# Recording the attention of both layers and emitting it on five engines in a planned order

## The chip, the core and the metric

The kernel runs on one core of one Trainium2 chip. The metric is the device time of one execution in microseconds (us). Before the change three runs took 1944.56, 1949.97 and 1951.2 us; their median is 1949.97 us. A fourth execution, taken with the hardware profiler, took 1945.29 us, and all rows of the trace come from it. The engines are TensorE (PE; its weight loads are shown as PEld), VectorE (DVE), ScalarE (ACT), GpSimd (POOL) and SyncE (SP), which issues the DMAs here.

## The reference, cut to what matters

Two layers of a trunk over 512 latent tokens and a prefix of 256 context tokens, with 1024 channels. In each layer:

```python
h  = modulate(rms_norm(x, norm1[l]), sh1, sc1)
na_q, na_k, na_v, gq, gk, gv, ga, gb = split(h @ w_in[l])     # one projection, eight parts
ya = na_latent(...)      # 8 heads: 8x16 windows on the 64-wide grid + all context keys, bias, softmax
yb = gqa_latent(...)     # 8 query heads on 2 key heads: rotary, normalised q and k, softmax over all keys
x  = x + g1 * ((sigmoid(ga) * (ya @ w_pa) + sigmoid(gb) * (yb @ w_pb)) @ w_o)
x  = x + g2 * swiglu(modulate(rms_norm(x, norm2[l]), sh2, sc2))
```

In the first layer the context tokens go through the same steps, with attention of their own; in the second layer they give keys and values alone.

## The kernel before, in words

Each fp32 operand is split in a high and a low half (`wh`/`wl` for weights, `h`/`hl` for activations, `pth`/`ptl` for transposed softmax weights), and each product is three matmuls. A weight block is loaded by SP into a ring of four buffers (`wr`, line 355), cast to `wh` on ACT (line 369) and subtracted to `wl` on GpSimd (line 371).

The attention stage of a layer is `mixing` (line 1385). It has a main thread, `attend` (line 1213), and fillers. The main thread goes through items; an item is two blocks of 128 queries of a head. Its steps are: scores (PE into the PSUM tile `sc`, one buffer of three banks), a minimum over each row (DVE, `TENSOR_REDUCE` at line 1048, or the fused add and minimum at line 1178 for windows), the exponential (ACT, line 1056 or 1180), the reciprocal of the row sum and the scaling (`soften`, lines 1009 and 1010, DVE), transposition (PE into `tp`), the split of the transposed tile (`split_t`: `pth` on ACT at line 1016, `ptl` on DVE at line 1017), the product with the values (PE into `y`), and its `join` (ACT line 1024, DVE line 1027). `tp`, `y`, `st` and `rb` share a PSUM ring of three buffers; the projections `pj` and `pv` have a ring of two. The fillers are the projections that the items and the later gates need: `na_q`, `na_k`, `na_v`, `gqa_q`, gates. Each ends in an evacuation of its PSUM tile by ACT and DVE, such as `sq`/`kg` (lines 815 and 816) or `qh`/`ql` (lines 990 and 991).

PE's order comes from the class `Flow` (line 148). While the program is being built, it walks the main thread, adds up PE's time in a clock, and lets fillers run until the time at which the main thread's next step is expected to be ready. The expected time comes from `Flow.go` (line 168), which books durations of the table `RATE` (line 96) on three lines for ACT, DVE and GpSimd. The instructions are issued to the framework at once. The whole stage stands in `manual_schedule(engines={PE})` (line 1516): PE keeps the order of issue, and the framework's own scheduler orders DVE, ACT, GpSimd and SP, across the stage and its neighbours. Each engine carries out its own instructions in order.

After the stage come `merge` (the gates, the products `pp` with `w_pa` and `w_pb`; its first operands `yb` are read back through DRAM and halved at lines 396 and 397), `out_proj`, and the feed-forward part, whose steps are ordered by hand on PE, DVE and ACT. The same merge computes modulation vectors beside its products (line 452, on `crow`, which line 444 and 445 prepare).

## Time and profile before

| | us |
|---|---|
| runs | 1944.56, 1949.97, 1951.2 (median 1949.97) |
| the profiled execution | 1945.29 |
| its span, first to last instruction | 1943.5 |
| PE busy | 1912.1 |
| attention stage of layer 0, about | 70 to 430 of the span |
| attention stage of layer 1, about | 1122 to 1452 of the span |

In rows of the profile, a matmul's duration overlaps the next one's, so an engine that is fed all the time shows 100% busy; "idle before" is the time between the end of the engine's last instruction and the start of this one, put down to the instruction that released it. Names stand as out<-in; L1017 is line 1017 of the kernel before.

### The profile page before, as it was taken

To read this page: it belongs to the slowest core of one execution; us is meant where nothing else is said; L and a number is where in the kernel's file an instruction comes from. 1 tells how busy PE (TensorE), PEld (TensorE's weight loads), DVE (VectorE), ACT (ScalarE), POOL (GpSimd) and SP (SyncE) were. 2 spreads that over 40 slices of the span, in tenths; PEclk is the share of its full clock that TensorE was granted. 3 is DMA by queue.
4 is the path that set the end of the run, shared out by engine and by line. 5 is a ranking of instruction groups with operands and counts; after the bars stand their busy time and mean duration, and the time that the engine had idled before them with its cause. 6 is when DMAs were issued, how large, how long until landed. Compare 5 with 4: busy or idle time off the path is not lost.

```text
span 1943.5 us, 31493 instructions
## 1 busy us (share of the span) xinstructions
PE 1912.1 (98%) x12298; PEld 1775.8 (91%) x12298; DVE 1470.0 (76%) x2802; ACT 943.0 (49%) x1822; POOL 226.6 (12%) x131
## 2 busy tenths in 40 slices
PE   8999999999999999999999998999999999999998
PEld 8989999998899999999999888889988999999998
DVE  7468887769877888786868577888657687877785
ACT  5466666652336533342424346666553355544553
POOL 0332222213300000000000012322300000000000
PEclk9999999999999999999999999999999999999999
DMA  8121112235562233334344411112235532332332
GB/s 328 44 65 48 47 64 63 77 105 182 170 217 87 66 120 122 117 116 133 131 141 143 143 62 55 47 60 64 73 102 173 201 109 77 98 120 88 103 97 83
DMA packets 71669, 210.85 MB, mean 108 GB/s; under 512 B 8544, under 2 KB 10720, under 8 KB 71520
## 3 DMA queue, kind: packets, MB, share of 16 engines
q1 hardware_dynamic: 71520, 208.84, 33.5%
q8 instruction: 96, 1.57, 0.3%
q14 instruction: 53, 0.43, 0.1%
HBM read 196.75 MB, written 6.82 MB: 105 GB/s over the span
## 4 chain that ended last, share of the span: by engine, by line
PE 69%; DVE 4%; issue 1%; ACT 1%; POOL 0%; DMA 0%; DVEq 0%; POOLq 0%; ACTq 0%
PE po L384 21%; PE qu L1740 14%; PE pj L384 11%; PE qv L1740 7%; PE pp L384 4%; PE qc L1740 3%; PE pf L384 3%; PE pv L957 1%; PE sc L1040 1%; PE y L1076 1%; PE tp L1066 1%; PE y L1203 1%; PE sc L1167 1%; PE tp L1191 1%; DVE m L1048 0%
## 5 line engine op out<-in xcount | busy, mean ns | idle before, releaser
L1740 PE MATMUL qu<-r,w 128*128 128x384 f32 (+1 forms) x1872 | 295.9, 310 | 0.3
L1740 PEld LDWEIGHTS qu<-r,w 128*128 128x128 f32 x1872 | 281.0, 190 | 4.9 <-DVE tt L2219 3.7
L384 PE MATMUL pj<-h,wh 128*128 128x512 f32 (+1 forms) x704 | 257.4, 366 | 3.3 <-ACT kg L816 1.7
L384 PE MATMUL pj<-h,wl 128*128 128x512 f32 (+1 forms) x704 | 247.6, 352 | 1.2 <-POOL wl L371 1.2
L384 PE MATMUL pj<-hl,wh 128*128 128x512 f32 (+1 forms) x704 | 247.0, 351 | 0.0
L369 ACT ACTIVATE wh<-wr 128x1024 fp32r<-128x1024 f32 (+1 forms) x131 | 124.6, 954 | 168.9 <-issue 43.5
L1603 ACT ACTIVATE w<-wr 128x512 fp32r<-128x512 f32 x234 | 145.4, 625 | 107.6 <-DVE wr L2183 36.1
L384 PE MATMUL po<-ph,wh 128*128 128x512 f32 (+1 forms) x576 | 197.5, 343 | 0.0
L384 PE MATMUL po<-ph,wl 128*128 128x512 f32 (+1 forms) x576 | 196.9, 342 | 0.0
L384 PE MATMUL po<-pl,wh 128*128 128x512 f32 (+1 forms) x576 | 196.3, 341 | 0.0
L371 POOL TENSOR_TENSOR wl<-wr,wh 128x1024 fp32r<-128x1024 f32 (+1 forms) x67 | 151.0, 2258 | 370.8 <-ACT wh L369 364.7
L1595 DVE SCALAR_TENSOR_TENSOR x<-po,G,x 128x256 f32<-128x256 f32 (+3 forms) x168 | 99.2, 596 | 101.0 <-PE po L384 100.0
L1607 DVE TENSOR_TENSOR w<-wr,w 128x512 fp32r<-128x512 f32 x234 | 159.4, 686 | 11.9 <-ACT w L1603 11.0
L384 PEld LDWEIGHTS pj<-h,wl 128*128 128x128 f32 x704 | 133.3, 189 | 19.7 <-POOL wl L371 1.6
L1740 PE MATMUL qv<-r,w 128*128 128x384 f32 (+1 forms) x936 | 150.7, 310 | 0.3 <-ACT tt L1746 0.3
L384 PEld LDWEIGHTS pj<-h,wh 128*128 128x128 f32 x704 | 133.7, 190 | 17.4 <-ACT kg L816 1.9
L384 PEld LDWEIGHTS pj<-hl,wh 128*128 128x128 f32 x704 | 134.0, 190 | 13.5
L1740 PEld LDWEIGHTS qv<-r,w 128*128 128x128 f32 x936 | 141.2, 190 | 0.5 <-ACT tt L1746 0.5
L1016 ACT ACTIVATE pth<-tp 128x512 fp32r<-128x512 f32 x176 | 103.2, 595 | 65.1 <-PE tp L1066 36.8
L512 POOL TENSOR_TENSOR rs<-rs,expo 128x2 f32<-128x2 f32 (+2 forms) x8 | 6.2, 773 | 1100.4 <-DVE rs L511 1100.4
L1017 DVE TENSOR_TENSOR ptl<-tp,pth 128x512 fp32r<-128x512 f32 x176 | 119.4, 684 | 18.4 <-ACT pth L1016 17.0
L384 PEld LDWEIGHTS po<-ph,wl 128*128 128x128 f32 x576 | 108.3, 188 | 14.3 <-DVE wl L1911 0.4
(255 smaller groups left out, 4325.2 us busy)
## 6 DMA issues: line engine op xcount, KB each, us to landing
wr<-wfi SPq DMA_DIRECT2D x88, 512.0 KB, 3.3
wr<-wmodT SPq DMA_DIRECT2D x84, 512.0 KB, 3.4
wr<-win SPq DMA_DIRECT2D x68, 512.0 KB, 3.3
wr<-wfo SPq DMA_DIRECT2D x64, 256.0 KB, 2.7
wr<-wo SPq DMA_DIRECT2D x26, 512.0 KB, 3.9
wr<-wp SPq DMA_DIRECT2D x32, 256.0 KB, 3.0
x<-x SPq DMA_DIRECT2D x16, 384.0 KB, 6.7
wr<-wmod SPq DMA_DIRECT2D x12, 512.0 KB, 7.6
```

Source lines behind the costliest of these rows:

```text
L369: nc.scalar.activation(hi, raw, AF.Copy)
L371: (eng or nc.gpsimd).tensor_tensor(lo, raw, hi[:].bitcast(F32), op=ALU.subtract)
L384: nc.tensor.matmul(ps[:, : b - a], u[:, c], v[k][:, a:b], start=(k == 0 and i == 0), stop=(k == nk - 1 and i == 2),)
L957: nc.tensor.matmul(ps[:, t * 256 : t * 256 + 256], a[k][:, tok], b[:, c], start=(k == 0 and i == 0), stop=(k == KB - 1 and i == 2))
L1016: nc.scalar.activation(hi, tp, AF.Copy)
L1017: nc.vector.tensor_tensor(lo, tp, hi[:].bitcast(F32), op=ALU.subtract)
L1040: nc.tensor.matmul(s[:, lo:up], qt[:, b * P : (b + 1) * P], kk[k][:, lo:up], start=(k == 0 and (b % 2 == 0 or lo > 0)), stop=(k == 1), ski ...
L1066: nc.tensor.transpose(tp[:, (2 * j + b) * P : (2 * j + b + 1) * P], ps_[b][:, (k + j) * P : (k + j + 1) * P], self.ident)
L1595: self.nc.vector.scalar_tensor_tensor(x[j][:, f:u], ps[:, f - a : u - a], self.G[l][i][:, s, j : j + 1], x[j][:, f:u], op0=ALU.mult, op1=A ...
L1603: self.nc.scalar.activation(t[:, :n], src, AF.Copy)
L1607: self.nc.vector.tensor_tensor(t[:, n : 2 * n], src, t[:, :n].bitcast(F32), op=ALU.subtract)
L1740: nc.tensor.matmul(banks[bank], u[:, c], v, start=(first and k == 0 and i == 0), stop=(k == kn - 1 and i == 2), skip_group_check=True)
```

## The change: what it does

For both layers (`all=True` in the table `PLAN`) the stage is first recorded and then emitted. While it is recorded, each call to an engine goes to `Plan.add`, which notes the instruction, its tiles, a duration from `Plan.cost` and which earlier instructions it has to follow. `Flow.go` now answers from the recorded ends. A tile in SBUF is compared by region; a tile in PSUM counts as one region, and all accesses to it by different engines keep the recorded order. `Plan.emit` then walks all recorded instructions: PE and SP keep their recorded order, while for ACT, DVE and GpSimd it takes among the instructions that can start first the one that is due first, where the due time is worked back from the PE instruction that needs it. It issues all of them by planned start, with five engines in `manual_schedule`. A scaling, subtraction or copy on DVE between SBUF tiles is not begun in the plan while GpSimd runs, and a GpSimd instruction is put off where such a DVE instruction is due earlier. The engines' instructions are the same in number, kind and shape. All instructions of the two stages bear line 541 in the changed kernel, since they are issued there.

The core of the diff:

```diff
-         busy=12, ctx=0.0, vat=(1, 1), load=2, qt=2, rx=2, slow=(1.1, 1.2, 1), banks="gst", lead=(2, 1, 2), quiet=0.0, spared=0),
+         busy=12, ctx=0.0, vat=(1, 1), load=2, qt=2, rx=2, slow=(1.1, 1.2, 1), banks="gst", lead=(2, 1, 2), quiet=0.0, spared=0, all=True),
...
     def go(self, t, *ops):
+        if self.plan:
+            return self.plan.go(t, ops)
...
+    def passed(self, v):
+        self.clock = max(self.clock + v, self.plan.pe if self.plan else 0.0)
...
+class Plan:
+    HOPS = dict(p=0.055, v=0.035, a=0.035, g=0.078, s=0.1)
+    TAIL = dict(p=-0.16, v=0.085, a=0.105, g=0.07, s=-2.2)
...
+    def go(self, t, ops):
+        flow, seen = self.flow, set()
+        for e, n in ops:
+            fixed, each, on = RATE[e]
+            if on in self.recent:
+                t = max(t, self.recent.pop(on))
+                seen.add(on)
+            elif on not in seen:
+                t += 0.05 + fixed + 0.08 + n * each
+        return t + flow.hop - 0.05
...
+    def region(ap, psum):
...
+        return (0, P, 0, 3 * S) if psum else (p, p + ap.ap[0][1], f, g)
...
+    def cost(self, lane, op, aps, kw, psum):
...
+        if lane == "s":
+            return n * aps[0].ap[0][1] * 4 / 0.34e6
+        if lane == "g":
+            return 0.31 if op == "memset" else 0.5 + n * 0.142 if n <= 16 else 0.14 + n * 0.0022
+        if lane == "a":
+            return 0.16 + n * 0.00088 + 0.08 * scaled + 0.1 * ("accum_out" in kw)
...
+        return 0.15 + n * (0.0006 if one else 0.00105) + 0.06 * (op == "scalar_tensor_tensor" and not psum)
...
+    def emit(self):
...
+        for i in reversed(range(n)):
+            o = ops[i]
+            due[i] = o["at"] if o["lane"] == "p" else min(
+                [due[j] - o["cost"] - 0.05 for j in then[i] + frees[i]], default=o["at"] + 15.0)
...
+            return max(t, clock["g"] - 0.07) if ops[i]["shared"] else t
...
+        for i in sorted(range(n), key=lambda i: (start[i], i)):
+            ops[i]["run"](*ops[i]["args"], **ops[i]["kw"])
...
-            with tc.manual_schedule(engines={mybir.EngineType.PE}):
+            if PLAN[l]["all"]:
+                nc.plan = flow.plan = Plan(flow)
                 flow.run(self.attend(items))
+                nc.plan = None
+                every = ("PE", "DVE", "Activation", "Pool", "SP")
+                with tc.manual_schedule(engines={getattr(mybir.EngineType, e) for e in every}):
+                    flow.plan.emit()
```

What stands where is shown at three places. The first is DVE in layer 1, where an item of the second query heads meets the evacuation of a key projection (`k<-pj`). `m<-sc` is the row minimum of one of the item's two blocks, `ptl` the split of a transposed tile of the item before. Before:

```order
L1017 TENSOR_TENSOR ptl_13250<-tp_13244,pth_13249 128x512
L936 TENSOR_TENSOR k_13321<-pj_13168,k_13321 64x512
L1048 TENSOR_REDUCE m_13271<-sc_13262 128x1
L1048 TENSOR_REDUCE m_13273<-sc_13262 128x1
L936 TENSOR_TENSOR k_13324<-pj_13168,k_13324 64x512
L1054 TENSOR_TENSOR m_13271<-m_13271,hr_12267 128x1
L1017 TENSOR_TENSOR ptl_13293<-tp_13287,pth_13292 128x512
L1054 TENSOR_TENSOR m_13273<-m_13273,hr_12267 128x1
```

and in the changed kernel, at the same projection (`k<-pj`, 64x512) of that layer:

```order
L541 TENSOR_TENSOR k_12124<-pj_12105,k_12124 64x512
L541 TENSOR_TENSOR q_12101<-qg_11985,q_12101 64x512
L541 TENSOR_TENSOR k_12125<-pj_12105,k_12125 64x512
L541 TENSOR_REDUCE m_12128<-sc_12127 128x1
L541 TENSOR_TENSOR ptl_12136<-tp_12134,pth_12135 128x512
L541 TENSOR_REDUCE m_12129<-sc_12127 128x1
L541 TENSOR_TENSOR m_12128<-m_12128,hr_12067 128x1
L541 TENSOR_TENSOR m_12129<-m_12129,hr_12067 128x1
L541 TENSOR_TENSOR y_12089<-y_12137,ys_12138 64x256
L541 TENSOR_TENSOR ptl_12141<-tp_12139,pth_12140 128x512
```

A `ptl` now stands between the two minima of an item, and the key's second half ahead of them; before, both minima and the key's second half stood ahead of the next `ptl`.

The second place is ACT at the beginning of layer 1, where the key projection of the context, `pj` 128x256, is evacuated by `sq` and `kg`. `wh` is the cast of a weight block for a later projection. Before:

```order
L1352 ACTIVATE kk_11969<-kg_11714 64x512 x2
L1352 ACTIVATE kk_11975<-kg_11714 64x512 x2
L369 ACTIVATE wh_11998<-wr_11996 128x1024
L990 ACTIVATE qh_12027<-pj_12002 64x448
L369 ACTIVATE wh_12104<-wr_12102 128x1024
L815 ACTIVATE sq_11715<-pj_12039 128x256
L816 ACTIVATE kg_11714<-pj_12039,gain_sb 128x256
L990 ACTIVATE qh_12027<-pj_12002 64x64
L990 ACTIVATE qh_12033<-pj_12002 64x448
```

and after:

```order
L541 ACTIVATE kk_11848<-kg_11714 64x512 x2
L541 ACTIVATE v_11812<-tv_11828 128x4x64
L541 ACTIVATE q_11851<-qg_11818 64x512
L541 ACTIVATE qh_11842<-pj_11841 64x448
L541 ACTIVATE wh_11839<-wr_11838 128x1024
L541 ACTIVATE qh_11842<-pj_11841 64x64
L541 ACTIVATE q_11852<-qg_11818 64x512
L541 ACTIVATE qh_11844<-pj_11841 64x448
L541 ACTIVATE sq_11715<-pj_11850 128x256
L541 ACTIVATE qh_11844<-pj_11841 64x64
L541 ACTIVATE kg_11714<-pj_11850,gain_sb 128x256
L541 ACTIVATE wh_11854<-wr_11853 128x1024
```

The two casts `wh` that stood right around the query halves have moved: one stays ahead of `sq`, the other is behind `kg`, and parts of `qh` and `q` stand ahead of `sq` instead.

The third place is DVE at the end of layer 0's stage, where the framework's own order takes over again. `y<-y` is the last join of the attention, `lo<-yb` halves the first operands of the merge, `junk` and `crow` prepare the modulation vectors. Before:

```order
L1027 TENSOR_TENSOR y_4757<-y_4989,ys_4994 64x256
L397 TENSOR_TENSOR lo_5113<-yb_5104,hi_5112 128x768
L397 TENSOR_TENSOR lo_5117<-yb_5106,hi_5116 128x768
L397 TENSOR_TENSOR lo_5121<-yb_5108,hi_5120 128x768
L397 TENSOR_TENSOR lo_5125<-yb_5110,hi_5124 128x768
L444 SCALAR_TENSOR_TENSOR junk_5170<-junk_5170,crow_5169 128x1024
L445 TENSOR_SCALAR crow_5169<-junk_5170 128x1024
L444 SCALAR_TENSOR_TENSOR junk_5170<-junk_5170,crow_5169 128x1024
L445 TENSOR_SCALAR crow_5169<-junk_5170 128x1024
L1585 SCALAR_TENSOR_TENSOR mb_5134<-gt_1454,pp_5135 128x512
```

and after:

```order
L541 TENSOR_TENSOR y_1500<-y_1548,ys_1549 64x256
L716 SCALAR_TENSOR_TENSOR junk_5170<-junk_5170,crow_5169 128x1024
L717 TENSOR_SCALAR crow_5169<-junk_5170 128x1024
L716 SCALAR_TENSOR_TENSOR junk_5170<-junk_5170,crow_5169 128x1024
L717 TENSOR_SCALAR crow_5169<-junk_5170 128x1024
L669 TENSOR_TENSOR lo_5113<-yb_5104,hi_5112 128x768
L724 ISA junk_5170,mod_105<-wr_5179,crow_5169 128x1024
L724 ISA mod_105 128x1
L669 TENSOR_TENSOR lo_5117<-yb_5106,hi_5116 128x768
L669 TENSOR_TENSOR lo_5121<-yb_5108,hi_5120 128x768
L724 ISA wr_5179,mod_105<-wr_5179,crow_5169 128x1024
L724 ISA mod_105 128x1
```

The four `lo<-yb` stood directly behind the last join; now the preparation of `crow` is ahead of all four, and modulation reductions (`ISA` into `mod`) stand between them, a further one and the fourth `lo` follow below the rows shown. On PE, 75 projection matmuls stood between the layer's last product with the values and the first `pp`; now 99 do, and the 24 more are of 512 columns.

## The prediction on record

> **What bounds the kernel now.** I read the page first, then the busy time of the stages, then PE's waits stage by stage, then the timeline around the longest ones. The page's head:
>
> ```profile
> span 1943.5 us, 31493 instructions
> PE 1912.1 (98%) x12298; PEld 1775.8 (91%) x12298; DVE 1470.0 (76%) x2802; ACT 943.0 (49%) x1822; POOL 226.6 (12%) x131
> ```
>
> PE is the bound, and an edit that only reorders cannot shorten its work. What it can take is PE's idle time, 1943.5 - 1912.1 = 31.4 us in the whole span, and of that only what lies in the two attention stages. The busy time by stretches, layer 0's attention, layer 1's, and for comparison the feed-forward part of layer 0 (columns: length, busy us of PE, PEld, DVE, ACT, POOL, granted clock, DMA):
>
> ```profile
> 70.00:430.00 360.00, 356.49 (x2494) 329.85 (x2493) 272.09 (x607) 220.34 (x475) 90.93 (x50) 1.00 0.21 64
> 1122.00:1452.00 330.00, 319.89 (x2091) 287.97 (x2090) 247.94 (x546) 194.55 (x397) 79.33 (x45) 0.99 0.21 64
> ...
> 633.00:1122.00 489.00, 488.63 (x2786) 463.70 (x2785) 379.12 (x647) 187.09 (x329) 1.01 (x1) 1.00 0.39 124
> ```
>
> PE is idle for 3.5 us in layer 0's attention and for 10.1 us in layer 1's: 13.6 us is what a better order there can win from waits. The feed-forward part, at a like load of DVE (379 of 489 us, against 272 of 360), idles 0.4 us: with an order that is written out on three engines a loaded DVE need not cost PE anything. PE's waits (us in total, times, longest), first seven of layer 1, then two of layer 0:
>
> ```profile
> PE sc L1040 <- ACT p L1056: 2.0, 2, 1.7
> PE tp L1066 <- DVE ptl L1017: 1.9, 1, 1.9
> PE pj L384 <- ACT kg L816: 1.7, 1, 1.7
> PE sc L1040 <- DVE kk L1353: 1.4, 1, 1.4
> PE y L1076 <- DVE ptl L1017: 1.0, 2, 0.8
> PE tp L1066 <- DVE p L1010: 0.8, 1, 0.8
> PE st L804 <- DVE y L1027: 0.7, 1, 0.7
> ...
> PE pj L384 <- DVE ql L991: 1.1, 2, 0.9
> PE tp L1191 <- DVE z L1010: 1.0, 1, 1.0
> ```
>
> No DMA and no GpSimd stands among the releasers of either stage. Each single wait is about the length of one or two instructions of DVE or ACT: an instruction that PE needed stood behind others in its engine's order.
>
> **Part by part: the order on DVE.** The longest wait, 1.9 us before a `tp`:
>
> ```profile
> 1281.17 1.82 DVE L1048 TENSOR_REDUCE m<-sc 128x1 f32<-128x768 f32 x2
> 1283.03 0.69 DVE L936 TENSOR_TENSOR k<-pj,k 64x512 fp32r<-64x512 f32 x1
> 1283.75 0.16 DVE L1054 TENSOR_TENSOR m<-m,hr 128x1 f32<-128x1 f32 x1
> 1283.94 0.69 DVE L1017 TENSOR_TENSOR ptl<-tp,pth 128x512 fp32r<-128x512 f32 x1
> ```
>
> The `ptl` that frees the PSUM buffer stands behind two minima and half a key, 1.82 + 0.69 + 0.16 = 2.7 us of DVE. In the changed order a `ptl` comes between the two minima, so behind one of them at most, 0.9 us instead of 2.7: 1.8 us earlier, and the 1.9 us go but for 0.1. The same pattern, a `ptl` behind a pair of minima, ends the `y` waits (1.0 us), and the order on DVE also sets `tp` on `p` and `st` on `y` (0.8 and 0.7). What is late next at these places is the score chain, since the second minimum waits for the `ptl`: 0.7 us later. That chain, minimum, `ptl`, minimum, scaling of the minimum, two exponentials, reciprocal, scaling, I add up from the rows above and these:
>
> ```profile
> L1010 DVE TENSOR_SCALAR p<-p,rc 128x768 f32<-128x768 f32 x32 | 20.5, 644 | 1.0
> L1009 DVE RECIPROCAL rc<-m 128x1 f32<-128x1 f32 x64 | 10.1, 159 | 10.9 <-ACT p L1056 8.3 <-ACT z L1180 1.9
> L1054 DVE TENSOR_TENSOR m<-m,hr 128x1 f32<-128x1 f32 x32 | 5.5, 182 | 0.1
> ...
> L1056 ACT ACTIVATE p<-sc,m,nr 128x768 f32<-128x768 f32 x32 | 31.6, 989 | 10.5 <-DVE m L1054 10.2
> ```
>
> 0.91 + 0.69 + 0.91 + 0.18 + 2 x 0.99 + 0.16 + 0.64 = 5.5 us, without the hops between engines (an estimate: half a us for all). Against that I counted the matmuls that PE's order puts between an item's last score and its first transposition, at the intervals of the trace:
>
> ```profile
> 100.00 0.39 PE L384 MATMUL pj<-h,wh 128*128 128x512 f32 x1
> 100.22 0.39 PE L384 MATMUL pj<-hl,wh 128*128 128x512 f32 x1
> ...
> 1282.38 0.28 PE L384 MATMUL pj<-hl,wh 128*128 128x256 f32 x1
> 1282.50 0.28 PE L384 MATMUL pj<-h,wl 128*128 128x256 f32 x1
> ```
>
> A start to the next is 0.23 us at 512 columns and 0.12 at 256 (I take 0.11 for 128). In layer 1 the items of the second kind of attention have 6.0 us at least and 7.4 in the median before, now 6.2 and 7.3; so the 6 us of the chain are just covered in both. In layer 0 their median falls from 7.9 to 6.9, and that of the window items from 6.7 to 5.3: PE's order has become tighter there, and I keep that for the rivals.
>
> **The order on ACT.** The wait of a `pj` on `kg`, 1.7 us:
>
> ```profile
> 1168.90 0.52 ACT L990 ACTIVATE qh<-pj 64x448 fp32r<-64x448 f32 x1
> 1170.65 1.06 ACT L369 ACTIVATE wh<-wr 128x1024 fp32r<-128x1024 f32 x1 [1.22 <-PE pj L384]
> 1171.61 0.37 ACT L815 ACTIVATE sq<-pj 128x256 f32<-128x256 f32 x1
> 1171.87 0.47 ACT L816 ACTIVATE kg<-pj,gain_sb 128x256 f32<-128x256 f32 x1
> ```
>
> A weight cast of 1.06 us for a later projection stood ahead of the two evacuations that PE was waiting for. Now that cast is behind them, while parts of `qh` and `q` (0.5 us each) are ahead: between nothing and 1.7 us is won, and I take 1.2. The two casts that are later delay GpSimd's `wl` by as much; their cover is the projection between, 24 matmuls of 0.12 to 0.23 us.
>
> **Recording, SP and GpSimd.** The instructions are the same, so nothing is added on any engine. SP's order changes too, but a load has one projection of lead before and after, and no PE wait of either stage ends on a DMA: nothing, with 1 us as the other end. GpSimd's multiplications still block DVE where both want SBUF: a pair of scalings takes 1.83 us at 348.4 while `bias` runs, though one takes 0.49 elsewhere, and two halves of a key 2.23 us at 1184.6 beside a rotary product `sh`.
>
> ```profile
> 348.37 1.83 DVE L1010 TENSOR_SCALAR z<-z,rc 128x512 f32<-128x512 f32 x1
> ...
> 1184.64 2.23 DVE L1353 TENSOR_TENSOR kk<-kg,kk 64x256 fp32r<-64x256 f32 x2
> ...
> 1382.13 0.49 DVE L1010 TENSOR_SCALAR z<-z,rc 128x512 f32<-128x512 f32 x1
> ```
>
> The plan puts a GpSimd instruction off in its own clock, but an order can only hold an instruction behind others of its engine; a GpSimd that is free starts as soon as its input is there. So the waits that come from it (`tp` on `z`, 1.0 us; `sc` on `kk`, 1.4) I let go only by half.
>
> **The seam after layer 0.** The last `lo<-yb` of the merge now has 2 x 1.2 + 2 x 0.7 us of `crow` and three reductions of 1.2 us ahead of it, 7.4 us more of DVE. Its cover has grown: 24 projection matmuls of 512 columns, 5.5 us, stand ahead of the first `pp`. On SP the two loads of `crow` are now ahead of the four of `yb`; a `crow` takes 8.5 us to land, and `yb` can be later by that at most, under the same cover. The difference on DVE, 1.9 us, is what this can cost, with 3 us (8.5 - 5.5) for the loads as the far end; the first `pp` needs the fourth operand only after three quarters of its matmuls, and I take nothing. The rows, the last one of the page's DMA issues:
>
> ```profile
> 423.84 1.21 DVE L444 SCALAR_TENSOR_TENSOR junk<-junk,crow 128x1024 f32<-128x1024 f32 x1
> 425.09 0.69 DVE L445 TENSOR_SCALAR crow<-junk 128x1024 f32<-128x1024 f32 x1
> ...
> 431.13 1.22 DVE L452 CUSTOM_DVE_ANT_0 junk<-wr,crow 128x1024 f32<-128x1024 f32 x1
> ...
> crow<-crow SPq DMA_DIRECT2D x3, 512.0 KB, 8.5
> ```
>
> **The clock.** Right behind the wait of 1.9 us the granted clock is at half from 1285.3 to 1288.7, 3.4 us:
>
> ```profile
> 1285.00:1286.00 1.00, 1.00 (x9) 1.00 (x7) 0.96 (x4) 1.00 (x4) 0.00 (x0) 0.71 0.00 0
> ...
> 1288.00:1289.00 1.00, 1.00 (x6) 0.96 (x6) 0.00 (x0) 0.00 (x0) 0.00 (x0) 0.59 0.00 0
> ```
>
> PE was busy then, so this is not in the 13.6 us; half of 3.4 is 1.7 us more, and it goes if the wait is its cause. The Trainium skill, in TensorE: Matmul & The Clock Gate, Part 1, has the clock fall to half after at least one idle window of about 3.4 us. No wait here is as long; by that rule the dip has another cause and stays, and the sum would be 1.7 us smaller.
>
> **The sum.** Idle now 13.6 us. Left over, at the low end the feed-forward part's rate (0.4 in 489, so 0.6 us in 690), at the high end layer 0's present rate in both stages (3.5 in 360, so 6.7 us). I take the middle, 3.6: the named terms above that stay (0.1 + 0.5 + half of 2.4) make 1.8, and as much again for new waits in the tighter layer 0. So 10.0 us go, with the clock 11.7: the profiled execution would take 1945.3 - 11.7 = 1933.6 us. The four executions shown average 1947.8 us, 2.5 above the profiled one, and I carry that along: 1936 us.
>
> **The rivals.** First, no change that can be told: a difference under 0.3% (5.85 us of 1949.97, about what a measurement of this kernel can tell from none). The waits named go, but others of the same length take their place, since DVE is as full as before and every item has two or three places where 1 us of delay reaches PE. For it: layer 0 idles 3.5 us now with longer covers than it will have. Against it: the changed order of DVE puts `ptl` first in general, 24 times directly behind a minimum where it was 6. With 4 us won the time is about 1944 to 1946 us. That the change does nothing is ruled out by the orders, which differ on all five engines throughout both stages.
>
> Second, slower, by one mechanism: layer 0's order of PE is built on recorded durations that hold only if no engine falls behind, and there GpSimd makes DVE fall behind. Layer 0's items have about 1 us less cover than before, and the mean of DVE's small scaling there already shows blocking:
>
> ```profile
> L1054 DVE TENSOR_TENSOR m<-m,hr 128x1 f32<-128x1 f32 x32 | 10.6, 340 | 0.0
> ```
>
> 340 ns against 182 in layer 1. If the chain of 6 us comes out at 7.6 on average, each of the 32 pairs of layer 0 waits for 0.7 us: 22 us in place of 3.5, against 8 to 9 us won in layer 1 with the clock. That gives 1947.8 + 18.5 - 8.5 = 1958 us. It decides from an average excess of 0.5 us per pair on. Against it speaks that PE's own wait shifts the whole order, and that the recorded durations agree with the rows (0.16 + 0.00088 x 768 + 0.26 = 1.1 us for an exponential with its sum, 0.99 and a read in the trace). The Trainium skill, in SBUF — State Buffer, Who interferes with whom, makes the port that DVE and GpSimd share an exclusive lock, held by whichever starts first; the rows above agree, and by that rule GpSimd would be held up as well, which the plan leaves out.
>
> **How the numbers follow.** Faster by over 0.3% (below 1944.1 us) 0.70: the orders show the cure at the places of the longest waits. Within 0.3% 0.18, slower 0.12. The likeliest case's own range is 1929 (all of 15.3 us gone from the lowest run, 1944.56) to 1943 (left over 6.7, clock unchanged, from the highest). To hold 8 in 10 it has to take in the case without change: 1929 to 1951.
>
> **What would show it.** Right: PE idle in the two stages down from 13.6 to about 3.6 us, the two minima of an item apart in DVE's timeline, no PE wait over 1 us in layer 1, no half clock there. The step on DVE is wrong if `tp` and `y` still wait on `ptl` for over 1 us; the one on ACT, if a `pj` waits on `kg`; the seam, if a `pp` waits on `lo`. The whole is wrong if layer 0's stage idles more than 10 us, with PE waiting on `p` or `z`.

## The result and the profile after

The changed kernel takes 1961.44 us in the median of 10 runs (1955.86 to 1964.02), the kernel before 1950.42 (1943.69 to 1955.17, 10 runs): ratio 1.0051, 95% interval 1.0037 to 1.0065. It is slower by half a per cent, where 1936 us and a gain were forecast. The runs of each kernel spread over 8 to 12 us, and each profile below is one execution, so a difference of a us or two between two profiles can be chance. The head of its page:

```profile
span 1955.7 us, 31538 instructions
PE 1918.5 (98%) x12298; PEld 1777.7 (91%) x12298; DVE 1477.4 (76%) x2802; ACT 944.4 (48%) x1822; POOL 227.3 (12%) x131
```

The span grew by 12.2 us, and of that PE shows 6.4 us as busy. The busy time by stretches: layer 0's attention, the seam behind it, layer 1's attention (columns as in the rows of before).

```profile
70.00:430.00 360.00, 347.74 (x2404) 318.48 (x2403) 266.39 (x600) 214.46 (x464) 89.22 (x48) 0.99 0.19 57
430.00:550.00 120.00, 120.00 (x692) 106.17 (x691) 101.59 (x151) 34.46 (x57) 41.67 (x21) 1.00 0.51 168
...
1122.00:1452.00 330.00, 323.31 (x2144) 292.07 (x2143) 256.87 (x549) 194.17 (x393) 80.22 (x46) 0.99 0.20 63
```

PE idles for 12.3 us in layer 0 (3.5 before) and for 6.7 in layer 1 (10.1 before). So layer 1 won a third of its idle time, and layer 0 lost more than twice that. PE's largest waits in layer 0, and then in layer 1 (us in total, times, longest):

```profile
PE tp L541 <- DVE z L541: 4.8, 3, 2.2
PE sc L541 <- ACT p L541: 3.3, 4, 1.4
PE sc L541 <- DVE m L541: 2.3, 2, 1.5
```

```profile
PE pj L541 <- ACT kg L541: 2.3, 1, 2.3
PE sc L541 <- ACT p L541: 1.6, 3, 0.9
PE tp L541 <- DVE z L541: 1.0, 1, 1.0
PE sc L541 <- DVE kk L541: 0.9, 1, 0.9
```

`ptl` is gone from both stages. In layer 0 the window items' scaling (`z`) has grown from 1.0 to 4.8 us, and the exponential (`p`) and the minimum (`m`) have come in. Below, "waits" are worked out from the trace in one way for all kernels: the time from a matmul's start to the next one's, less the usual interval at its width, where it exceeds that by over 0.2 us, added up over the stage. That gives 4.5 us for layer 0 and 12.2 for layer 1 before, 15.5 and 8.9 after. The time at half clock (the spells at the very start and end of the span, which most profiles have, left out) went from 3.4 to 10.2 us, and half of that is time lost: 3.4 us more. Together 11.0 - 3.3 + 3.4 = 11.1 of the 12.2 us.

**What layer 0 waits for.** SyncE's timeline in the middle of layer 0, changed kernel (start, us, operation):

```profile
240.12 0.37 SPq L541 DMA_DIRECT2D wr<-win  x1
240.58 0.42 SPq L541 DMA_DIRECT2D bias<-rpb  x1
249.41 0.47 SPq L541 DMA_DIRECT2D qh<-qh  x1
257.77 0.46 SPq L541 DMA_DIRECT2D ql<-ql  x1
260.75 0.46 SPq L541 DMA_DIRECT2D qh<-qh  x1
261.31 1.44 SPq L541 DMA_DIRECT2D ql<-ql  x1
271.31 0.33 SPq L541 DMA_DIRECT2D yd<-y  x1
271.73 0.38 SPq L541 DMA_DIRECT2D wr<-win  x1
272.20 0.43 SPq L541 DMA_DIRECT2D bias<-rpb  x1
272.72 0.46 SPq L541 DMA_DIRECT2D wr<-win  x1
273.24 0.42 SPq L541 DMA_DIRECT2D bias<-rpb  x1
```

For 31 us no weight and no bias is loaded, because SyncE stands at the copies `qh`, `ql` and at the store `yd<-y`, each of which waits for its data. When the store is through, four loads go out within 2 us. What SyncE waits for over the stage says the same. After, the two largest (waits for `wl` come to 13.8 there):

```profile
SPq L541 <- ACT qh L541: 136.0, 6, 47.1
SPq L541 <- DVE y L541: 123.1, 4, 40.9
```

Before, `wl` is first (a load waits until the subtraction has freed its buffer in the ring, so it is as early as it can be), and the copies and stores come to 30.7 and 24.7:

```profile
SPq L360 <- POOL wl L371: 165.7, 17, 19.5
SPq L1001 <- ACT qh L990: 30.7, 5, 11.2
...
SPq L1477 <- DVE y L1027: 24.7, 4, 12.7
```

What the bunch does, on GpSimd, DVE and PE of the changed kernel (rows picked out):

```profile
277.16 2.40 POOL L541 TENSOR_TENSOR wl<-wr,wh 128x1024 fp32r<-128x1024 f32 x1 [25.74 <-ACT wh L541]
279.51 1.86 POOL L541 TENSOR_TENSOR bias<-bias 128x768 f32<-128x768 f32 x1
280.89 0.69 DVE L541 TENSOR_TENSOR k<-pj,k 64x512 fp32r<-64x512 f32 x1 [0.88 <-ACT k L541]
281.57 2.36 POOL L541 TENSOR_TENSOR wl<-wr,wh 128x1024 fp32r<-128x1024 f32 x1
281.62 0.69 DVE L541 CUSTOM_DVE_ANT_1 z<-sc,bias 128x512 f32<-128x512 f32 x1
283.08 0.47 PE L541 MATMUL sc<-k,qh 128*128 128x256 f32 x2 [1.54 <-DVE m L541]
283.89 1.81 POOL L541 TENSOR_TENSOR bias<-bias 128x768 f32<-128x768 f32 x1
283.99 4.73 DVE L541 TENSOR_SCALAR z<-z,rc 128x512 f32<-128x512 f32 x2
285.66 2.53 POOL L541 TENSOR_TENSOR wl<-wr,wh 128x1024 fp32r<-128x1024 f32 x1
286.13 0.41 PE L541 MATMUL tp<-ident_sb,z 128*128 128x128 f32 x2 [1.67 <-DVE z L541]
288.77 0.69 PE L541 MATMUL tp<-ident_sb,z 128*128 128x128 f32 x2 [2.23 <-DVE z L541]
```

GpSimd had nothing to do for 25.7 us and then worked for 13 almost without a pause. The minimum (`z<-sc,bias`) starts on DVE at 281.6, and the scores behind it wait for 1.7 us. Two things end just ahead of it: its `bias` on GpSimd, at 281.4, and half a key (`k<-pj`) that the plan put in front of it on DVE, at 281.6; runs below tell them apart. Then two scalings take 4.73 us where two take 1.0 elsewhere in this stage, one beside `bias` and one beside `wl`, and each is followed by a wait of PE. The stretch costs three waits of 1.7, 1.9 and 2.4 us (as counted above), and the clock is at half from 287.6 to 294.4, from within the third wait on.

A late load reaches PE plainly further on. A load of `bias` goes out at 387.8, right behind four copies of `qh` and `ql`:

```profile
392.93 1.84 POOL L541 TENSOR_TENSOR bias<-bias 128x768 f32<-128x768 f32 x1 [33.95 <-DMA bias<-rpb]
394.81 0.69 DVE L541 CUSTOM_DVE_ANT_1 z<-sc,bias 128x512 f32<-128x512 f32 x1 [4.63 <-POOL bias L541]
```

GpSimd is idle for 34 us until it lands, DVE waits for GpSimd, and PE waits 0.9 us for the minimum at 396.

### The profile page after: what moved, and what is told of

Same layout as the page of the kernel before. It is cut to its first block, busy times and chain, and to the rows that moved or that the text cites. A ratio compares the mean times of both kernels' runs of the same rounds, so it can differ in the third digit from the quotient of the medians.

```text
span 1955.7 us, 31538 instructions
## 1 busy us (share of the span) xinstructions
PE 1918.5 (98%) x12298; PEld 1777.7 (91%) x12298; DVE 1477.4 (76%) x2802; ACT 944.4 (48%) x1822; POOL 227.3 (12%) x131
## 4 chain that ended last, share of the span: by engine, by line
PE 63%; DVE 5%; issue 2%; ACT 1%; DMA 1%; POOL 0%; SPq 0%; DVEq 0%; POOLq 0%; ACTq 0%
PE po L656 21%; PE qu L2035 14%; PE qv L2035 7%; PE pj L541 4%; PE qc L2035 3%; PE pj L656 3%; PE pf L656 3%; PE pp L656 2%; PE sc L541 2%; PE y L541 2%; PE tp L541 1%; PE pv L541 1%; ACT p L541 1%; DVE m L541 1%; DVE ptl L541 0%
## 5 line engine op out<-in xcount | busy, mean ns | idle before, releaser
L541 PE MATMUL pj<-h,wh 128*128 128x512 f32 (+1 forms) x512 | 188.8, 369 | 3.4 <-ACT kg L541 2.3
L541 PE MATMUL pj<-h,wl 128*128 128x512 f32 (+1 forms) x512 | 179.1, 350 | 0.0
L541 PE MATMUL pj<-hl,wh 128*128 128x512 f32 (+1 forms) x512 | 179.0, 350 | 0.0
L1902 DVE TENSOR_TENSOR w<-wr,w 128x512 fp32r<-128x512 f32 x234 | 159.6, 687 | 12.0 <-ACT w L1898 11.1
L541 POOL TENSOR_TENSOR wl<-wr,wh 128x1024 fp32r<-128x1024 f32 x44 | 107.5, 2446 | 230.4 <-ACT wh L541 230.3
L641 ACT ACTIVATE wh<-wr 128x1024 fp32r<-128x1024 f32 (+1 forms) x85 | 75.9, 898 | 117.8 <-PE po L656 29.1
L656 PEld LDWEIGHTS po<-pl,wh 128*128 128x128 f32 x576 | 108.7, 189 | 12.7
L656 PEld LDWEIGHTS po<-ph,wh 128*128 128x128 f32 x576 | 108.7, 189 | 12.6
L541 PEld LDWEIGHTS pj<-h,wl 128*128 128x128 f32 x512 | 97.8, 191 | 12.6
```

The source lines that it names most:

```text
L541: ops[i]["run"](*ops[i]["args"], **ops[i]["kw"])
L641: nc.scalar.activation(hi, raw, AF.Copy)
L656: nc.tensor.matmul(ps[:, : b - a], u[:, c], v[k][:, a:b], start=(k == 0 and i == 0), stop=(k == nk - 1 and i == 2),)
L1902: self.nc.vector.tensor_tensor(t[:, n : 2 * n], src, t[:, :n].bitcast(F32), op=ALU.subtract)
```

## The experiments

Ratios are to runs of the kernel before on the same chip, with their 95% intervals. The runs come from several chips, on which the kernel before took 1948.9 to 1951.4 us, so a difference in us between the medians of two versions can be a us or two off what their ratios give.

**Which layer.** The change in one layer alone, by its own switch:

```diff
-         ... quiet=0.0, spared=0, all=True),
+         ... quiet=0.0, spared=0, all=False),
```

> Recording and planned order in layer 1 alone; layer 0 as before. From the two traces layer 0's attention lost 11 us of PE waits (4.5 to 15.5) and layer 1's won 3.7 (12.6 to 8.9), and the half-clock time grew from 3.4 to 10.2 us (3.4 us of time), nearly all of the growth in layer 0. If the loss sits in layer 0 alone: 1950.4 - 3.7 = about 1947 us, ratio 0.998, with layer 1's waits at 8 to 10 us and layer 0's at 4 to 5. If instead both stages were made worse and layer 1's gain is an accident of one profile: 1950 or more.

> The same for layer 0 alone. If the stages add: 1950.4 + 11 + 3.4 = about 1965 us, ratio 1.0075, layer 0's waits near 15 us and two half-clock spells or one long one. If the two layers don't add (the second stage begins in another state of the queues): anything else, near 1961.

Layer 1 alone: 1949.49 us, 0.9987 (0.9971 to 1.0003), waits 4.4 us in layer 0 and 9.7 in layer 1. Layer 0 alone: 1963.18 us, 1.0069 (1.0049 to 1.0089), waits 15.7 and 12.9, 17 us at half clock. The loss is layer 0's; layer 1's gain is smaller than expected and can't be told from none. The two ratios add up to +0.56%, against +0.51% for both. (The first expectation puts layer 1 at 12.6 us before; counted as above it is 12.2.) In the profile of layer 1 alone PE also idles for 5.8 of the 203 us behind layer 0, where it was 1.6 before, and that is more than layer 1's waits fell.

**SyncE given back.** The order of PE, DVE, ACT and GpSimd is that of the changed kernel, row for row:

```diff
-                every = ("PE", "DVE", "Activation", "Pool", "SP")
+                every = ("PE", "DVE", "Activation", "Pool")
```

> The changed kernel with SyncE alone given back to the framework's scheduler in both stages; PE, DVE, ACT and GpSimd keep the planned order row for row. Theory one (SyncE in recorded order: loads of weights and bias stand behind stores and copies that wait up to 47 us for ACT or DVE, then come in a bunch, so GpSimd works for 13 us without a break beside the softmax and makes the bias late): the waits at 281 to 287 and at 395 us go, 7 of layer 0's 15.5 us, with the half-clock spell there (3.4 us): 1950 to 1953 us. Theory two (PE's recorded order leaves the softmax too little cover, whoever loads when): within 2 us of 1961. Theory three (GpSimd blocks DVE, but not by the order of loads): 1958 to 1962.

1956.51 us, 1.0034 (1.0020 to 1.0048); layer 0's waits fall to 11.4, with one half-clock spell of 3.4 us in the attention. So SyncE's order alone, with the others as they were planned, is worth 5 us (3 by the ratios), where theory one asked for 8 to 11. The waits at 281 to 287 us shrank from 6.0 to 2.7. What is left there is in the planned order of the others: the bias of that item is now loaded at 220.7 us, but GpSimd still does it behind a `wl` that starts at 278.2, after 25.3 us of nothing to do. Even so it ends 1.2 us before the minimum starts; the minimum stands behind half a key on DVE, and the 1.7 us behind it are unchanged.

**GpSimd's length.** `wl` is cut to 128 of its 1024 columns, and the low halves of the others are left out; in the changed kernel, and as a control in the kernel before:

```diff
-        (eng or nc.gpsimd).tensor_tensor(lo, raw, hi[:].bitcast(F32), op=ALU.subtract)
+        if short:
+            lo = lo[:, 0:P]
+        c = slice(0, P if short else cols)
+        (eng or nc.gpsimd).tensor_tensor(lo, raw[:, c], hi[:, c].bitcast(F32), op=ALU.subtract)
...
```

> The changed kernel with GpSimd's subtraction for the low half of a projection weight cut to 128 of 1024 columns (the products use these 128 columns for all blocks, so the low halves of the other columns are left out); all five engines keep their order in the attention stages. Each wl should take 0.4 instead of 2.4 us. If GpSimd is the cause (theories one and three): of layer 0's 15.5 us, the 11.7 us with a GpSimd instruction in the chain ahead of them go but for 2, the half-clock spells go (5 us), layer 1 wins 2: about 1945 us. Theory two (too little cover): 1957 or more, layer 0's waits above 12 us.

> The kernel before with the same cut of GpSimd's wl to 128 columns (low halves of the other columns left out), as the control of the run with the changed kernel, which came to 1944.4 us. The waits of before with a GpSimd instruction in their chain are 1.2 us in layer 0 and about 3 in layer 1, and one half-clock spell of 3.4 us stands behind one that has none. If GpSimd hurts the changed kernel more than the kernel before: 1945 to 1948 us here, that is 3 to 6 won against 17 there. If it hurts both alike: 1934.

Changed: 1944.39 us, 0.9969 (0.9958 to 0.9980), layer 0's waits 8.2, layer 1's 6.2, and one half-clock spell of 3.4 us is left. Before: 1939.37 us, 0.9946 (0.9928 to 0.9964), waits 3.3 and 9.2. The theory that PE's cover alone decides falls: 17 us go with GpSimd's length. But the control wins 11.6 us and lies between its two cases (1945 to 1948, or 1934). So GpSimd's `wl` is dear in both kernels, and only 5.4 us of it are the change's own. The load behind the copies is as late as ever in the shortened kernel (it goes out at 380.6, DVE waits 4.5 us and PE 0.8), so it was not GpSimd's length that made it late. The wait of 1.7 us, now at 282, stays too, though its `bias` is done 2.5 us before the minimum starts: it comes from the half key that DVE's planned order puts ahead of the minimum, not from the bias.

**PE's order against the others'.** First the order of before on PE with the rest planned, then the order of the changed kernel on PE with the rest left to the scheduler:

```diff
-                nc.plan = flow.plan = Plan(flow)
+                nc.plan = rec = Plan(flow)
...
-                    flow.plan.emit()
+                    rec.emit()
```

(with lines of its own for the plan's bookings, so that the recording does not move PE)

```diff
-                every = ("PE", "DVE", "Activation", "Pool", "SP")
+                every = ("PE",)
```

> PE's order row for row that of the kernel before; DVE, ACT, GpSimd and SyncE in the order that the plan works out for it. If PE's new order is the cause (less cover): layer 0's waits 4 to 6 us, time 1945 to 1951. If the planned order of the other engines is the cause, with GpSimd's bunches: layer 0's waits 10 us or more, time 1956 to 1962.

> The other half: PE in the order of the changed kernel, all other engines given back to the framework's scheduler. If PE's new order is the cause: layer 0's waits 10 us or more, time 1956 or more (the free order knows nothing of the plan's, so up to 1970). If the planned engines are: 1947 to 1952.

1972.14 us, 1.0110 (1.0090 to 1.0130), waits 11.2 and 19.2; and 1965.84 us, 1.0085 (1.0064 to 1.0106), waits 16.9 and 12.4. Each half is slower alone than both together, and each run came out as the case that blames the half of the change that it kept (waits of 10 us or more in layer 0), so the two don't tell the halves apart. For the planned half with the old PE order a cause was still open here: SyncE, or DVE and ACT.

**SyncE in the plan.** PE's order is that of the changed kernel, row for row, but SyncE takes in the plan what is due first among what can start. The plan then places the others anew around it: in the two attention stages 36 of 1120 rows on DVE, 40 of 839 on ACT and 14 of 95 on GpSimd stand elsewhere.

```diff
-        queue = {e: [i for i, o in enumerate(ops) if o["lane"] == e] for e in "ps"}
-        can = {e: {i for i, o in enumerate(ops) if o["lane"] == e and not left[i]} for e in "avg"}
+        queue = {"p": [i for i, o in enumerate(ops) if o["lane"] == "p"]}
+        can = {e: {i for i, o in enumerate(ops) if o["lane"] == e and not left[i]} for e in "avgs"}
```

> The changed kernel with SyncE put among the engines that take in the plan what is due first among what can start, instead of keeping the recorded order. PE keeps its order; DVE and ACT move by a few rows. SyncE left free gave 1956.5 us, 5 less than the changed kernel. If what is gained there comes from loads no longer standing behind stores: the same here, 1954 to 1958, with layer 0's waits near 11 us. If the plan places GpSimd better once it knows the loads: 1950 or less.

1946.42 us, 0.9983 (0.9969 to 0.9997): 15 us faster than the changed kernel (13 by the ratios) and ahead of the kernel before. Its stages, and SyncE's two largest waits with the stores' row:

```profile
70.00:430.00 360.00, 353.37 (x2461) 323.54 (x2461) 268.59 (x609) 218.04 (x474) 92.70 (x50) 1.00 0.21 64
...
1122.00:1452.00 330.00, 325.00 (x2168) 294.41 (x2167) 254.31 (x552) 196.99 (x399) 80.35 (x46) 1.00 0.22 68
```

```profile
SPq L541 <- POOL wl L541: 171.4, 19, 20.9
SPq L541 <- ACT qh L541: 39.9, 7, 12.7
...
SPq L541 <- DVE y L541: 23.6, 4, 13.0
```

The ring is first again, as before the change, and copies and stores are at 39.9 and 23.6. Layer 0's waits are 9.1 us, layer 1's 6.6, and no half clock is left in either stage. The wait behind the minimum near 280 is gone. This is the second of the two cases expected: not 5 us as with SyncE free, but 15, for SyncE's order together with the rows that the plan moved on the others.

**SyncE's order by itself.** The kernel before, with nothing planned:

```diff
-            with tc.manual_schedule(engines={mybir.EngineType.PE}):
+            with tc.manual_schedule(engines={mybir.EngineType.PE, mybir.EngineType.SP}):
                 flow.run(self.attend(items))
```

> The kernel before with one change: SyncE, too, keeps the order in which the program issues its instructions through both attention stages (PE's order is unchanged row for row; the scheduler moves DVE, ACT and GpSimd by a few rows). Theory: the recorded order of SyncE alone does the harm, since loads of weights and bias stand behind copies and stores that wait for ACT or DVE. Then layer 0's waits rise from 4.5 to 9 us or more and the time to 1957 to 1965. Rival: it does harm only with the planned order of the others, which have no slack: within 3 us of 1951.

1987.79 us, 1.0187 (1.0167 to 1.0208): 36 us, more than either case expected. Its stages and SyncE's largest waits in layer 0:

```profile
70.00:430.00 360.00, 347.45 (x2397) 321.32 (x2396) 262.61 (x596) 211.70 (x461) 89.50 (x49) 0.98 0.17 56
1122.00:1452.00 330.00, 310.59 (x1991) 277.94 (x1990) 237.18 (x503) 179.16 (x359) 71.71 (x42) 0.97 0.17 56
```

```profile
SPq L1477 <- DVE y L1027: 166.0, 4, 47.3
SPq L1001 <- ACT qh L990: 88.3, 3, 44.3
```

The same signature as in the changed kernel, larger. Waits are 14.6 us in layer 0 (4.5 before) and 25.9 in layer 1 (12.2), and 41 us are at half clock. In neither stage does a wait of PE end on a DMA here either. SyncE's order of issue is enough by itself (the scheduler moves the others by a few rows). The changed kernel, whose PE order and other engines were planned around it, lost less.

**What the rest of the plan is worth.** With SyncE planned: in layer 1 alone (the switch above); `wl` on DVE in place of GpSimd; `wl` cut as above:

```diff
-        return self.weight(self.d["win"][l, BLOCK[what, j]], D, self.nc.vector if first else None)
+        return self.weight(self.d["win"][l, BLOCK[what, j]], D, self.nc.vector)
```

> SyncE planned, but recording and plan in layer 1 alone; layer 0 as before. If the stages add up: layer 0's waits 4.5 us as before, layer 1's 6.6 as with SyncE planned (12.2 before), one half-clock spell less: 1951 - 5.6 - 1.7 = about 1944, ratio 0.996. If layer 0's part of the plan was no loss any more: 1946 or more.

> SyncE planned, and the low halves of the projection weights subtracted on DVE instead of GpSimd, in both layers; nothing is left out. GpSimd keeps the bias and one rotary product. DVE gets 44 subtractions of about 1.2 us, 53 us more in 690. If GpSimd's hold on DVE's operands costs more than that work: layer 0's waits about 5 us, 1938 to 1943. If a fuller DVE delays the softmax as much: 1947 or more.

> SyncE planned, with wl on GpSimd cut to 128 of 1024 columns (the other columns' low halves left out). SyncE's order and GpSimd's length as two separate losses: 1946.4 less the 11.6 us that the cut won in the kernel before, so 1935 to 1938. If the bunches were what made GpSimd costly, so that one of the two cures is enough: 1942 to 1945.

Layer 1 alone: 1943.79 us, 0.9958 (0.9946 to 0.9970), waits 4.4 and 6.6 as expected. It is the fastest version that computes everything, 18 us ahead of the changed kernel. On DVE: 1948.20 us, 0.9987 (0.9975 to 1.0000), waits 10.1 and 6.8; DVE's busy time in layer 0 rises from 268.6 to 283.6 us, so what GpSimd no longer blocks, the fuller DVE seems to delay. Cut: 1940.01 us, 0.9944 (0.9927 to 0.9962). So GpSimd's length is worth 6.4 us (8 by the ratios) once SyncE is planned, against 17.0 in the changed kernel and 11.6 before: the bunches and its length are not two separate losses, and not one either.

**What is left in layer 0.** PE in the order of before with all four others planned (SyncE too), and the plan with a larger allowance per step in layer 0:

```diff
-         early=0.9, reserve=8, hop=0.14, move=3.5, ...
+         early=0.9, reserve=8, hop=0.5, move=3.5, ...
```

> PE in the order of the kernel before, the other four planned, now with SyncE among those that are planned (with SyncE in recorded order it was 1972 us). If SyncE's order made the 21 us there too: 1948 to 1953, layer 0's waits 4 to 6 us. If the plan's order of DVE, ACT and GpSimd is at fault with this order of PE: 1958 or more. Layer 0's waits tell what is left of the loss there: 4 to 6 us says that PE's new order costs the rest of it (9.1 against 4.5), 9 or more says that the planned DVE and ACT do.

> SyncE planned, and for layer 0 the allowance that the recording adds to each expected time set from 0.14 to 0.5 us, so that PE's order puts more projection matmuls between a score and what needs its softmax. If short cover is what remains of layer 0's loss: its waits fall from 9.1 to 6 us, 1943 to 1945. If not: 1945 to 1948, or more, since fillers run out earlier.

> The same with 0.9 us. Short cover: layer 0's waits 4 to 5 us, 1942 to 1944. Otherwise as with 0.5 us, or slower by the fillers that are missing at the end of the stage.

PE before, all planned: 1948.12 us, 0.9996 (0.9983 to 1.0009), waits 7.0 and 10.2. With SyncE in recorded order it was 1972, so SyncE's order, with what the plan makes of it on the others, made the 24 us there as well. Layer 0's 7.0 us lie between the two cases (4 to 6, or 9 and more): of the 4.6 us by which its waits with all planned (9.1) exceed those of before, about half come with the planned order of the others and half with PE's, from one profile each. Allowance 0.5: 1948.49 us, 0.9992 (0.9979 to 1.0005), layer 0's waits 6.1. Allowance 0.9: 1947.47 us, 0.9986 (0.9975 to 0.9997), waits 5.0. The waits fall as the theory of short cover says, from 9.1 to 5.0, and the time does not. In the profiles, what the stage wins is lost behind it; first SyncE planned with 0.14 in the 203 us behind layer 0's stage, then with 0.9 in the stage and behind it:

```profile
430.00:633.00 203.00, 201.51 (x1165) 185.83 (x1164) 164.13 (x262) 70.19 (x113) 43.08 (x23) 1.00 0.48 164
```

```profile
70.00:430.00 360.00, 356.63 (x2486) 328.01 (x2485) 266.51 (x607) 219.91 (x475) 91.29 (x50) 1.00 0.20 64
430.00:633.00 203.00, 196.99 (x1136) 181.69 (x1135) 167.92 (x270) 69.08 (x115) 41.71 (x22) 1.00 0.48 161
```

PE idles for 1.5 us there in the one and for 6.0 in the other, on a `wl` of DVE (2.7 us), on `mh`, `t` and a `wl` of GpSimd (1.0 to 1.2 each). Why those are later was not tried. It need not be the allowance: with layer 1 alone planned, where layer 0 is as before, the profiles idle for 5.8 us (SyncE as recorded) and 4.7 us (SyncE planned) in these 203 us, the largest part on a `wl` of DVE as well.

The cases side by side, as ratios to the kernel before:

| | others free | others planned, SyncE as recorded | all planned |
|---|---|---|---|
| PE's order of before | 1 | 1.0110 | 0.9996 |
| PE's order of the change | 1.0085 | 1.0051 | 0.9983 |
| PE's order of before, SyncE as issued | 1.0187 | | |

## Why the prediction was wrong

- **The step that failed** is the one on SyncE: "SP's order changes too, but a load has one projection of lead before and after, and no PE wait of either stage ends on a DMA: nothing, with 1 us as the other end." It is worth 13 to 15 us (1961.4 to 1946.4 with SyncE planned, PE's order the same and a few rows of the others moved), 3 to 5 of them with the others left as they were planned, and 36 us by itself in the kernel before. I judged it by whether PE waited on a DMA. It never does in the two stages after either; the delay reaches PE by way of ACT's casts, GpSimd's bunch and the scalings that it blocks, and once by a late bias. What SyncE itself waits for was left out, where the rows of before already showed loads bound by the ring and not by stores.
- **DVE's order in layer 1** was right: no `tp` and no `y` waits on `ptl` any more, and layer 1's waits fell, from 12.2 us to 8.9 with the recorded SyncE and 6.6 with the planned one. The forecast left 3.6 us in both stages together.
- **ACT's order** was wrong. The `pj` on `kg` waits for 2.3 us, not 0.5. The cast moved away as read, but a part of `qh` in front of `sq` and `kg` waits for `ql`, which DVE does behind `kk` the first time and behind a `wl` the second:

```profile
1183.92 1.05 ACT L541 ACTIVATE wh<-wr 128x1024 fp32r<-128x1024 f32 x1
1185.39 0.22 ACT L541 ACTIVATE qh<-pj 64x64 fp32r<-64x64 f32 x1 [0.42 <-DVE ql L541]
...
1187.68 0.22 ACT L541 ACTIVATE qh<-pj 64x64 fp32r<-64x64 f32 x1 [0.45 <-DVE ql L541]
1187.92 0.47 ACT L541 ACTIVATE kg<-pj,gain_sb 128x256 f32<-128x256 f32 x1
```

  All accesses of different engines to a PSUM tile keep their recorded order, so `qh`, `ql`, `qh`, `ql` on the two halves of one `pj` go by turns, and two hand-overs between ACT and DVE of 0.4 us each stand ahead of `kg`.
- **GpSimd** was read rightly (an order can't hold an idle engine back; waits that come from it stay), but sized at half of 2.4 us. Its `wl` is worth 11.6 us in the kernel before and 17 in the changed one. The row quoted for a pair of scalings (1.83 us at 348.4) is that of a single one (x1), so the blocking was larger than it was read. GpSimd itself was hardly held up: the 41 `wl` of 1024 columns that the changed kernel does in its two stages took 2.36 to 2.93 us, 2.40 in the median.
- **The seam** was right: PE is busy for 120.00 of 120 us behind layer 0, and no `pp` waits.
- **The clock** was right in that the spell behind the `ptl` wait went with it (the window ahead of it had held 1.9 us without a matmul); it was missed that others would come. The last section has what decides.
- **The rival that ended slower** gave 1958 us, with GpSimd holding DVE up in layer 0, and the sign that "layer 0's stage idles more than 10 us, with PE waiting on `p` or `z`" came (12.3 us, on `z`, `p`, `m`). Its reason for why that starts to hurt, shorter cover, is the smaller part: 4 us of waits hang on it, and no time that could be told, so that its number came close is in part luck. The larger part is that loads came in bunches. I gave it too little chance because the recorded durations agreed with the rows; where GpSimd blocked DVE they did not hold (2.0 and 2.8 us for a scaling of 0.5), and the bunch that set them side by side came from a queue that the plan keeps in recorded order.
- **What the idea itself is worth.** With SyncE planned, layer 1 wins 5.6 us of waits and 1.7 of clock, and layer 0 loses 4.6: 2.7 us from one profile each, 3.3 by the ratio (0.17% of 1950). The forecast of 10 us from waits was too high even then, since layer 0 had only 3.5 us of idle time to give and the plan's orders, PE's and the others', opened new waits there.
- **A bound** of the likeliest case was added up wrongly: 1943 us follows from the median (1949.97 less 6.9), while the highest run, 1951.2, that it names gives 1944.3.

## What to carry to other kernels

An engine that only issues DMAs is part of the order: if it carries loads and also copies or stores that wait for results, writing its instructions in program order puts the loads behind the results, even if no wait of the bound engine ever names a DMA. Read what the DMA queue itself waits for: ring buffers coming free is what one wants, results of the engines is what one doesn't. And when an order on many engines is changed at once, give one engine back at a time; here one run named the engine, and a gain of the idea hidden behind it could be had.

## What the runs showed of the hardware

**Which waits cost clock.** The wait of `pj` on `kg`, 2.3 us, is there in ten of the profiles at the same place; in three of them the clock fell to half behind it, in seven not. Going through the 17 profiled executions, all changes to half clock begin on borders of windows of 3.413 us that run on through the execution (in the changed kernel the two spells in the attention start 264.0 such windows apart; in the run with SyncE as issued nine spells in and between the stages all lie within 0.05 of whole numbers). For each window at full clock, the first 20 and the last 25 us of a span left out, I added up the time without a matmul. With 1.89 us or more of 3.41 the next window was at half clock in 24 cases of 24; from 1.5 to 1.89 us in 7 of 26; from 0.7 to 1.5 in 1 of 118; below that in none of 3753. So it is not a wait's length that counts, but how much of it, with its neighbours, falls into one window. What decides between 1.5 and 1.89 us these traces don't show. The stretch of the changed kernel (PE's busy time is the first number behind the length, the granted clock the third from the end):

```profile
287.00:288.00 1.00, 0.00 (x0) 0.00 (x0) 1.00 (x1) 0.00 (x0) 1.00 (x1) 0.79 0.00 0
...
289.00:290.00 1.00, 1.00 (x6) 1.00 (x6) 0.93 (x4) 0.65 (x2) 1.00 (x1) 0.50 0.00 0
```

The window from 284.2 to 287.6 held 2.7 us without a matmul; the clock is half from its end on, also once PE is busy again. The Trainium skill, in TensorE: Matmul & The Clock Gate, Part 1, says that such a window of 3413 ns is free-running, and the spacing here agrees. It gives one idle window as the condition for the half clock; here a window that is a little over half idle was enough, and the measurement decides.

**Small operations are blocked too.** Beside a `wl`, a DVE multiplication of two 128x1 tiles took up to 2.10 us and one of two 128x2 tiles 2.16, where the median of their kind in the stage is 0.15:

```profile
L541 DVE TENSOR_TENSOR m<-m,hr x40: 137/154/2155, 97.5 to 258.5; 128x1 f32<-128x1 f32 x32, 128x2 f32<-128x2 f32 x8
```

It stands between the minimum and the exponential, so GpSimd's 2.4 us can land in the chain whatever the operation's size. With `wl` cut to 128 columns, none of the 40 took over 0.34 us in the changed kernel.
